# A hybrid decoder step on one Trainium2 core: up-projection of 19 tile pairs by seven products of quarters

## The chip, the core and the metric

The kernel runs on one core of one Trainium2 chip. The engines' names here are those of the profile: PE is the matrix engine (PEld its weight loads), DVE the vector engine, ACT the activation engine, POOL the general engine, SP the engine that issues most of the DMAs. The metric is device time in microseconds (us). The kernel before takes 2202.07 us, the median of three runs (2200.95 to 2202.59).

## The reference

One layer of a decoder trunk is computed for two groups of requests that share weights: a prompt of 1024 tokens and eight samples of one token each. All is float32, the model width is 1024, the feed-forward width FF is 2816. Cut to the part that changes:

```python
def conv_ffn(x, buf, w_up, conv_w, conv_b, w_down):
    L = x.shape[1]
    hup = x @ w_up                                  # 1024 -> 5632
    ext = concatenate([buf, hup], axis=1)
    c = ext[:, 0:L]*conv_w[0] + ext[:, 1:L+1]*conv_w[1] + ext[:, 2:L+2]*conv_w[2] + conv_b
    a, b = split(c, 2, axis=-1)                     # 2816 and 2816
    return (gelu(a) * b) @ w_down, ext[:, -2:]

x = layer_norm(ALPHA*x + mix)                       # mix: mLSTM, pooling and memory attention, gated, @ w_o
f, cbuf_new = conv_ffn(x, cbuf, ...)
x = layer_norm(ALPHA*x + f)
```

Ahead of it stand the memory's keys and values, one input projection with a chunked mLSTM, causal pooling and cross-attention, three gated output projections and the projection `w_o`. The prompt's and the samples' new states are outputs too, among them the last rows of `hup`.

## The kernel before

Activations lie transposed, features on the 128 partitions and TT = 1032 tokens (1024 of the prompt, 8 samples) along a row. Each float32 number is held as a high part that the matrix engine takes in full and a low part with the rest: the normalised stream is `xhi` and `xlo`, eight tiles of 128 features each. A product of two such numbers takes three matmuls (high x high, high x low, low x high).

The main work is a list of `Unit`s. A unit makes 128 output features: for each of three token chunks (`CHUNKS`, 384, 384 and 264 columns) it adds `nk` x 3 matmuls into one PSUM bank at L250 and then calls `evac`, which takes the result out. Weights come as `Split`s of 512 KB: `load` fetches one on SP's queue into a `raw` buffer (L171), `split_part` makes its high part on ACT (L180) and its low part on DVE or POOL (L181), in two halves. `raw` has two buffers, `whi` and `wlo` three each. `run_units` writes the order of all this out by hand: it counts an estimated time per matmul, puts weight halves between matmuls (`tick`), and lets side work (generators in two lanes of `Side`, and `post`, the rest of a unit's evacuation) advance by the same clock. The order in which instructions are written is the order on each engine.

Lines that the texts below touch: L366 is a small step of the layer norms on POOL, L384 to L387 (`to_features`) normalise into `xhi` and `xlo`, L1106 and L1127 store gate and attention chunks to DRAM from POOL's queue, L1375 and L1379 (`wo_unit`) add the stream to the output projection, L1392 transposes that back into rows.

In the feed-forward part an `up_unit` makes one of 44 tiles of 128 columns of `x @ w_up`. ACT writes the rows to `hup` (L1479) and, scaled, to `cv` (L1480). Four steps on DVE add the two other taps of the convolution (L1492, two over the prompt, two over the samples). The first half of the columns then goes through the gelu (L1495), the second half is multiplied with it on POOL (L1498), and the gated row is split into high and low parts (`GH`), which stay in on-chip memory. The up-projection runs by two tiles at a time. The down-projection is cut into groups of four gated rows (`down(j0, 4)`), which are put between the up-units as the rows become ready; each adds into `Z2` (L1533). The last group of four goes by three passes over the tokens (`PASSES`), and the last layer norm (L1597 to L1619) follows each pass.

The tile pool `rows` (`H`, 21 buffers of 1032 columns) holds nearly all larger intermediate tiles. Two kinds of PSUM buffers exist: five of tag `s` (`PS`) and three of tag `d`.

Of the kernel before, what the change touches and what calls it, by code (L numbers as in the profile page):

```python
# [15 lines left out]
T = 1024  # L16
# [13 lines left out]
NEG = -1e30  # L30

# [75 lines left out]
def tile_hybrid_step(ctx: ExitStack, tc: tile.TileContext, x_prompt, mem_prompt, x_sample, cache_mem_k,  # L107
# [9 lines left out]
    wp = ctx.enter_context(tc.tile_pool(name="weights", bufs=2))  # L117
    hp = ctx.enter_context(tc.tile_pool(name="rows", bufs=NH))
# [64 lines left out]
    def run_units(first_loads):  # L183
# [80 lines left out]
        flush()  # L264
# [84 lines left out]
    sp = ctx.enter_context(tc.tile_pool(name="small", bufs=4))  # L349

# [26 lines left out]
    def to_features(rows, c0, n, g0, b0, wait, per=1):  # L377

        for f in range(8):
# [6 lines left out]
            nc.vector.tensor_copy(xhi[:, f, c0:c0 + n], tmp[:, :n])  # L386
# [713 lines left out]
    def gate_unit(b, f, split, col, spill):  # L1100
        def evac(ci, c0, n, p):
            bias = bias_in(GT0 + 8 * b + f)
            if spill:
                t = chunk_tile()
                nc.scalar.activation(t[:, :n], p[:, :n], AF.Identity, bias=bias)  # L1105
                nc.gpsimd.dma_start(GD[b][f][:, c0:c0 + n], t[:, :n])  # L1106
# [16 lines left out]
    def xo1_unit(f, split, col):  # L1123
        def evac(ci, c0, n, p):
            t = chunk_tile()
            nc.scalar.activation(t[:, :n], p[:, :n], AF.Copy)
            nc.gpsimd.dma_start(y1D[f][:, c0:c0 + n], t[:, :n])  # L1127
        return Unit(split, col, 4, mov_o(0), evac)

    def xo2_unit(f, split, col):  # L1130
# [5 lines left out]
        def evac(ci, c0, n, p):  # L1136
# [3 lines left out]
            if ci == 2:  # L1140
                nc.gpsimd.dma_start(mixD[0][f], Y1.pop(f))
# [221 lines left out]
    Z = {}  # L1363
# [4 lines left out]
    def wo_unit(chunk, tiles, f, split, col):  # L1368
        def evac(ci, c0, n, p):
            if tiles[-1] not in Z:  # L1370
                for t in tiles:
                    Z[t] = H(f"z{t}")[:, :1024].rearrange("p (f t) -> p f t", f=8) if t < 8 else \
                        cur[0].tile([128, 8, NS], F32, tag="zs", bufs=1, name="zs")
            tmp = cur[0].tile([128, 392], F32, tag="tmp", bufs=3, name=nm("ztmp"))
            nc.vector.scalar_tensor_tensor(tmp[:, :n], raw_f(xhi[:, f, c0:c0 + n]), ALPHA, p[:, :n], op0=OP.mult,  # L1375
                                           op1=OP.add)
            for t in tiles:
                a, m = t * 128, rows_of(t)
                nc.vector.scalar_tensor_tensor(Z[t][:, f, :], raw_f(xlo[:, f, a:a + m]), ALPHA,  # L1379
                                               tmp[:, a - c0:a - c0 + m], op0=OP.mult, op1=OP.add)  # L1380
        return Unit(split, col, 8, mov_mix, evac, chunks=(chunk,))

    XN = {}

    def g_rows1(tiles):
        st = {}
        for i in range(len(tiles) + 1):
            if i < len(tiles):
                t, m = tiles[i], rows_of(tiles[i])
                p = [PS(), PS()]  # L1390
                for f in range(8):
                    nc.tensor.transpose(p[f // 4][:m, (f % 4) * 128:(f % 4 + 1) * 128], Z[t][:, f, :], ident)  # L1392
                st[t] = p, *ln_stats([q[:m] for q in p], m)
                Z.pop(t)
# [12 lines left out]
    def few_to_features(rows):  # L1407
# [4 lines left out]
        for f in range(8):  # L1412
            nc.scalar.activation(tmp[:, f], p[:, f * NS:(f + 1) * NS], AF.Identity,
                                 bias=colA[:, L1B + f:L1B + f + 1], scale=colA[:, L1G + f:L1G + f + 1])
        nc.vector.tensor_copy(xhi[:, :, T:], tmp)
        nc.vector.tensor_sub(xlo[:, :, T:], tmp, raw_f(xhi[:, :, T:]))

    def g_ln1(tiles):
# [4 lines left out]
        yield from to_features([(XN[t], 128) for t in tiles], tiles[0] * 128, len(tiles) * 128, L1G, L1B, 1.5)  # L1423
# [4 lines left out]
    for i, (chunk, tiles) in enumerate(PASSES):  # L1428
        pairs = list(enumerate(weight_pairs(w_o[0], 0, 1024)))[::-1 if i % 2 else 1]
        for j, (f, sc) in enumerate(pairs):  # L1430
            if i == 0 or j >= NW:
                wo[f] = sc
                sc[0].pool = i+j>1 and (i < 2 or j % 3)
# [3 lines left out]
        on(units[-1], "after", lambda t=tiles, i=i: (side.add(0, f"rows1{i}", g_rows1(t)),  # L1437
# [4 lines left out]
    CA, GH, RW = {}, {}, {}  # L1442
    Z2 = {}
    STT = {}
    TL = {}

    def g_state_conv():

        stT = STT[0] = H("stT")[:, :704].rearrange("p (f j b) -> p f j b", f=44, j=2)
# [8 lines left out]
        for q, (n, t) in enumerate(rows):  # L1458
# [3 lines left out]
            nc.vector.tensor_copy(stT[:, q * 8:q * 8 + n].rearrange("p f j b -> p (f j b)"), p[:, :n * 16])  # L1462
# [219 lines left out]
```

## Time and profile before

| | |
|---|---|
| median of three runs | 2202.07 us |
| the profiled execution, its own time | 2202.02 us |
| its span, first to last instruction | 2200.3 us |
| busy: PE, DVE, ACT, POOL | 2159.7, 1170.9, 797.5, 362.1 us |
| mean granted clock of the matrix engine | 0.995 |
| moved by DMA, mean rate | 229.52 MB, 104 GB/s |

Busy shares are of the whole span. A row of a group of instructions gives the line, engine, operation, what it writes and reads, the shapes, how many there are, their busy time and the mean of one in ns, then the idle time of the engine just ahead of them with what ended it. A row of the timeline gives start and duration in us, and in brackets the idle time ahead and what ended it. Matmuls start before the one ahead of them has drained, so the distance from start to start is what one takes of the engine's time.

### The profile page before, as it was taken

How to read it: one execution, taken by the hardware profiler on the slowest of the kernel's cores; microseconds unless marked ns; L12 is line 12 of the kernel's file. 1: busy time of each engine (PE TensorE's matmuls, PEld its weight loads, DVE VectorE, ACT ScalarE, POOL GpSimd, SP SyncE). 2: the span in 40 equal slices, each digit the busy share in tenths (PEclk: the TensorE clock that was granted, in tenths of full speed). 3: DMA queues.
4: the chain of work that ended last, by engine and by line, in shares of the span. 5: the costliest groups of instructions: out<-in, count | busy, mean ns of one | idle time of the engine just before them, and what ended most of it. 6: DMA issues, size and time to landing. Idle time of an engine off the chain costs nothing.

```text
span 2200.3 us, 35980 instructions
## 1 busy us (share of the span) xinstructions
PE 2159.7 (98%) x14345; PEld 2118.7 (96%) x14345; DVE 1170.9 (53%) x2692; ACT 797.5 (36%) x1583; POOL 362.1 (16%) x523
## 2 busy tenths in 40 slices
PE   8999999999999999999999999999999999999996
PEld 7899999999998999999999999999999999999996
DVE  6844838383856654524335556745544343443457
ACT  5524343434445533332213333544142331423411
POOL 6301010101110000111004633101010110101104
PEclk9999999999999999999999999999999999999998
DMA  8231232323268665659543232311111111111112
GB/s 256 65 107 53 54 69 62 63 53 79 87 175 271 192 207 183 202 184 349 184 140 122 68 88 76 87 49 49 49 39 52 46 49 48 39 58 40 49 49 78
DMA packets 268948, 229.52 MB, mean 104 GB/s; under 512 B 15797, under 2 KB 245991, under 8 KB 268763
## 3 DMA queue, kind: packets, MB, share of 16 engines
q1 hardware_dynamic: 262443, 208.12, 32.0%
q0 software_dynamic: 6336, 19.09, 2.3%
q8 instruction: 113, 1.85, 0.4%
q14 instruction: 56, 0.46, 0.1%
HBM read 177.13 MB, written 50.64 MB: 104 GB/s over the span
## 4 chain that ended last, share of the span: by engine, by line
PE 87%; DVE 4%; issue 4%; POOL 3%; DMA 1%; ACT 1%; SPq 0%; POOLq 0%; ACTq 0%; DVEq 0%
PE pd L250 78%; PE ps L669 2%; PE ps L668 1%; PE ps L670 1%; POOL ps L1276 1%; DVE xlo L387 1%; PE ps L692 1%; DMA Cs<-in_state_C_dram 1%; PE ps L382 0%; DVE xhi L386 0%; PE ps L873 0%; PE ps L1072 0%; DVE st L358 0%; DMA x<-in_x_prompt_dram 0%; POOL mx L1325 0%
## 5 line engine op out<-in xcount | busy, mean ns | idle before, releaser
L250 PE MATMUL pd<-xhi,whi 128*128 128x384 f32 (+1 forms) x2784 | 898.7, 323 | 0.7 <-ACT gf L541 0.7
L250 PE MATMUL pd<-xlo,whi 128*128 128x384 f32 (+1 forms) x2784 | 894.6, 321 | 0.0
L250 PE MATMUL pd<-xhi,wlo 128*128 128x384 f32 (+1 forms) x2784 | 891.1, 320 | 0.0
L250 PEld LDWEIGHTS pd<-xhi,whi 128*128 128x128 f32 x2784 | 523.8, 188 | 10.3 <-issue 8.3
L250 PEld LDWEIGHTS pd<-xlo,whi 128*128 128x128 f32 x2784 | 524.2, 188 | 1.8 <-issue 1.7
L250 PEld LDWEIGHTS pd<-xhi,wlo 128*128 128x128 f32 x2784 | 523.6, 188 | 1.8 <-issue 1.7
L181 DVE TENSOR_TENSOR wlo<-raw,whi 128x512 fp32r<-128x512 f32 (+1 forms) x326 | 227.0, 731 | 440.7 <-ACT whi L180 432.7
L180 ACT ACTIVATE whi<-raw 128x512 fp32r<-128x512 f32 (+1 forms) x382 | 219.3, 619 | 275.8 <-PE pd L250 206.0
L1479 ACT ACTIVATE hup<-pd 128x384 f32<-128x384 f32 (+1 forms) x132 | 60.5, 458 | 276.5 <-PE pd L250 276.4
L1492 DVE SCALAR_TENSOR_TENSOR cv<-hup,colB,cv 128x1023 f32<-128x1023 f32 x88 | 112.7, 1281 | 1.6
L1533 DVE TENSOR_TENSOR z<-pd,z 128x384 f32<-128x384 f32 (+3 forms) x120 | 59.6, 511 | 82.5 <-PE pd L250 82.5
L366 POOL TENSOR_TENSOR rs<-rs,half 128x1 f32<-128x1 f32 (+2 forms) x60 | 38.0, 633 | 340.8 <-DVE rs L365 331.8
L1489 POOL COPY tl<-hup 128x10 f32<-128x10 f32 x44 | 8.4, 192 | 519.2 <-ACT hup L1479 519.2
L1480 ACT ACTIVATE cv<-pd,colB 128x384 f32<-128x384 f32 (+1 forms) x132 | 83.6, 633 | 0.0
L181 POOL TENSOR_TENSOR wlo<-raw,whi 128x512 fp32r<-128x512 f32 x56 | 76.3, 1386 | 41.7 <-ACT whi L180 41.7
L1106 POOL DMA_DIRECT2D gD<-ch x60 | 32.8, 547 | 287.7 <-ACT ch L1105 268.0
L1498 POOL TENSOR_TENSOR cv<-cv,cv 128x1032 f32<-128x1032 f32 x22 | 53.2, 2418 | 112.5 <-DVE cv L1492 96.9
L250 PE MATMUL pd<-mh,whi 128*128 128x392 f32 (+2 forms) x192 | 62.6, 326 | 0.6 <-ACT mh L1327 0.6
L250 PE MATMUL pd<-ml,whi 128*128 128x392 f32 (+2 forms) x192 | 62.0, 323 | 0.1
L1105 ACT ACTIVATE ch<-pd,colA 128x384 f32<-128x384 f32 (+1 forms) x60 | 32.8, 546 | 79.5 <-PE pd L250 59.8
L250 PE MATMUL pd<-mh,wlo 128*128 128x392 f32 (+2 forms) x192 | 61.5, 320 | 0.0
L662 ACT ACTIVATE hh<-ps,colA 128x128 fp32r<-128x128 f32 x64 | 23.1, 361 | 79.7 <-DVE hh L663 75.1
(724 smaller groups left out, 3926.6 us busy)
## 6 DMA issues: line engine op xcount, KB each, us to landing
raw<-in_w_in_dram SPq DMA_DIRECT2D x72, 512.0 KB
raw<-in_w_up_dram SPq DMA_DIRECT2D x44, 512.0 KB
raw<-in_w_down_dram SPq DMA_DIRECT2D x22, 512.0 KB
raw<-in_w_o_dram SPq DMA_DIRECT2D x18, 512.0 KB
mx<-mixD SPq DMA_DIRECT2D x16, 516.0 KB
raw<-in_w_mem_kv_dram SPq DMA_DIRECT2D x16, 512.0 KB
Cs<-in_state_C_dram SPq DMA_DIRECT2D x32, 256.0 KB
out_dram<-Cs SPq DMA_DIRECT2D x32, 256.0 KB
```

The costliest lines, as they stand in the source:

```text
L180: nc.scalar.activation(s.hi[:, ks], s.raw[:, ks], AF.Copy)
L181: (nc.gpsimd if s.pool else nc.vector).tensor_sub(s.lo[:, ks], s.raw[:, ks], raw_f(s.hi[:, ks]))
L250: nc.tensor.matmul(p[:u.m, :n], lhsT=a, rhs=b, start=j == 0, stop=j == len(seq) - 1)
L366: nc.gpsimd.tensor_tensor(out=rs[:n], in0=rs[:n], in1=half[:n], op=OP.pow)
L669: nc.tensor.matmul(out, lhsT=wh, rhs=xl, start=False, stop=False)
L1105: nc.scalar.activation(t[:, :n], p[:, :n], AF.Identity, bias=bias)
L1106: nc.gpsimd.dma_start(GD[b][f][:, c0:c0 + n], t[:, :n])
L1479: nc.scalar.activation(rw[:, c0:c0 + n], p[:, :n], AF.Copy)
L1480: nc.scalar.activation(cc[:, c0:c0 + n], p[:, :n], AF.Identity, bias=colB[:, 132 + ft:133 + ft], scale=colB[:, 88 + ft:89 + ft])
L1492: nc.vector.scalar_tensor_tensor(a, b[0], b[1], a, op0=OP.mult, op1=OP.add)
L1498: nc.gpsimd.tensor_mul(cc, CA.pop(j), cc)
L1533: nc.vector.tensor_add(Z2[f][:, cs], p[:, :n], Z2[f][:, cs])
```

## The change

The up-projection of the first three pairs of column tiles stays as it is. A pair is a tile of the gelu half and the tile of the other half at the same place. For the other 19 pairs the product of a pair is taken as a 2 x 2 block product: the activations in four quarters (512 features x 516 tokens each), the pair's weights in four quarters (512 features x 128 columns). Seven products of sums of quarters take the place of eight products of quarters; the results are put together in PSUM, by adding products onto a bank (`onto`), and on DVE.

- The three sums of activation quarters that the stream itself doesn't hold (products 6, 7, 4) and one that replaces a quarter of it (product 5) are formed once by `g_parts` and `last_part`, from a copy of the normalised stream that `to_features` now also spills to DRAM (`x1D`).
- The sums of weight quarters are formed per pair by DMA: SP loads the first quarter of a sum, and POOL issues accumulating DMAs for the others onto the same tile (`load_weights`): two for product 6, one for 7, one for 5, three for 3. Twelve such tiles exist. `prepare` splits a finished one (256 KB) into high and low parts in one of up to ten buffers.
- `run_pairs` runs the products of half the tokens at a time in the order `ORDER`, with the third and fourth product of a half put among those of the next; `conv_pair` is the convolution of a pair, in seven steps.
- Gated rows go to DRAM (`gD`) and are read back. The down-projection runs as one block after all pairs, in groups of the same sizes as before, with the gated rows of two groups at a time in `xhi` and `xlo`. The residual is read back from `x1D`.
- Ahead of the feed-forward part: weights and raw buffers share one tag of eight buffers; the weights of `w_o` are all split on DVE; the stream's sum in `wo_unit` takes two steps per tile and chunk; the high part in `to_features` moves from DVE to ACT; the stores of gate and attention chunks and the small loads move from POOL's queue to ACT's, one more from POOL's to SP's. The DMA scratch of POOL's queue is 4096 bytes instead of the default.

The core of the diff:

```diff
+NSTD = 3
+SEQ = (1, 2, 6, 7, 5, 3, 4)
+HB, HT = 258, 516
+NWF = 12
...
-    wp = ctx.enter_context(tc.tile_pool(name="weights", bufs=2))
-    hp = ctx.enter_context(tc.tile_pool(name="rows", bufs=NH))
+    wp = ctx.enter_context(tc.tile_pool(name="weights", bufs=8, side="right"))
+    hp = early.enter_context(tc.tile_pool(name="rows", bufs=NH))
...
-            nc.vector.tensor_copy(xhi[:, f, c0:c0 + n], tmp[:, :n])
+            if spill:
+                nc.scalar.dma_start(spill[f][:, c0:c0 + n], tmp[:, :n])
+            nc.scalar.activation(xhi[:, f, c0:c0 + n], tmp[:, :n], AF.Copy)
...
+    def load_weights():
+        for d, chain in list(chains):
+            nc.gpsimd.dma_start(d, chain.pop(0), accum_op=OP.add)
+            if not chain:
+                chains.remove((d, chain))
+        while made["load"] < len(wq) and made["live"] < NWF:
+            o = wq[made["load"]]
+            key = o.steps[made["key"]]
+            first, *chain = o.src[key]
+            o.f[key] = wf_tile(first.shape[1] * 128)
+            d = o.f[key].rearrange("p (k c) -> p k c", c=128)
+            nc.sync.dma_start(d, first)
+            if chain:
+                chains.append((d, chain))
+            made["live"] += 1
...
+    def prepare():
...
+        if key not in o.f or any(d.tensor is o.f[key].tensor for d, _ in chains):
+            return False
+        slot = slots.pop(0)
+        t = (wp if slot == "w" else place["ex"]).tile([128, 1024], F32R, tag="w", name=nm("whl"))
...
+        nc.scalar.activation(hi, src, AF.Copy)
+        nc.vector.tensor_sub(lo, src, raw_f(hi))
...
+        load_weights()
+        return True
...
+            src = {1: (a11,), 2: (a12,), 6: (a21, a22, a11), 7: (a11, a21), 5: (a21, a22),
+                   3: (a12, a21, a22, a11), 4: (a22,)}
...
+        def product(self, m):
+            u = self.u
+            ready_weights(u.w, m)
+            onto = {6: 1, 5: 1, 3: 1, 4: 7}.get(m)
+            if onto is None:
+                self.bank[m] = pp.tile([128, 512], F32, tag="d", bufs=3, name=nm("pd")) if m == 1 else PS("pd")
+            p = self.bank[onto or m][:, :HB]
+            wh, wl = u.w.w[m][:2]
+            for k in range(4):
+                xh, xl = x_part(m, k, self.s)
+                for n, (a, b) in enumerate(((wh, xh), (wh, xl), (wl, xh))):
+                    nc.tensor.matmul(p, lhsT=a[:, k], rhs=b, start=onto is None and k + n == 0,
+                                     stop=k == 3 and n == 2, skip_group_check=onto is not None)
+            if self.s:
+                release(u.w, m)
+            if m in (1, 6, 5):
+                t = small({1: "t1", 6: "u2", 5: "v"}[m])
+                nc.scalar.activation(t, p, AF.Copy)
+                setattr(self, f"s{m}", t)
+            elif m == 2:
+                nc.vector.tensor_add(self.rows(0)[:, self.c1], p, self.s1)
+            elif m == 3:
+                nc.scalar.activation(self.rows(0)[:, self.c2], p, AF.Copy)
+            elif m == 4:
+                nc.vector.scalar_tensor_tensor(self.rows(1)[:, self.c1], p, -1.0, self.s6, op0=OP.mult, op1=OP.subtract)
+        def c22(self):
+            nc.vector.scalar_tensor_tensor(self.rows(1)[:, self.c2], self.bank[7][:, :HB], -1.0, self.s5, op0=OP.mult,
+                                           op1=OP.subtract)
...
+    ORDER = ((1, 0), (2, 0), (3, 1), (6, 0), (4, 1), (7, 0), (5, 0))
+    def run_pairs():
+        before = None
+        halves_ = [Half(u, s) for u in pairs for s in range(2)]
+        for i, h in enumerate(halves_ + [None]):
...
+            for x, (m, old) in enumerate(ORDER):
+                hh = before if old else h
+                if hh is None:
+                    continue
+                hh.product(m)
+                if before and (x == 0 or h is None and m == 3):
+                    before.c22()
+                if m == 4 and hh.s:
+                    post.append(conv_pair(hh.u.j, hh.u.out))
+                if x in (2, 3, 5, 6):
+                    post[:] = [g for g in post if next(g, g) is not g]
+                if x in (0, 1, 4) or x == 3 and h and h.s:
+                    if not prepare():
+                        load_weights()
+                if i == len(halves_) - 1:
+                    early_stage(m)
+                side.advance(12 * HB / 2180.0)
+            before = h
...
+    def stage_split(gi, k, c0, c1):
+        kk = (gi % 2) * 4 + k
+        nc.scalar.activation(xhi[:, kk, c0:c1], stage[gi][:, k, c0:c1], AF.Copy)
+        nc.vector.tensor_sub(xlo[:, kk, c0:c1], stage[gi][:, k, c0:c1], raw_f(xhi[:, kk, c0:c1]))
...
+    pairs = [Pair(j) for j in range(NSTD, NFF)]
...
     run_units(2)
+    made["open"] = True
+    side.finish("parts")
+    slots.extend("www")
+    last_part()
+    load_weights()
+    run_pairs()
+    for u in downs:
+        run_down(u)
+    flush()
...
-    nc = _bacc.Bacc("TRN2", target_bir_lowering=False, num_devices=1)
+    nc = _bacc.Bacc("TRN2", target_bir_lowering=False, num_devices=1, dynamic_dma_scratch_size=4096)
```

Not shown: `early_stage` reads the first four gated rows back during the last half of the last pair, in pieces of 516 columns, and splits them into `xhi` and `xlo`, four while its last products run and four behind the last one that reads those columns; `g_stages` loads and splits the later groups; `run_down` has the same matmuls per group as `down_unit` before.

More of the change, by code (lines that the diff above doesn't have):

```diff
@@ L1414, in few_to_features @@
                                  bias=colA[:, L1B + f:L1B + f + 1], scale=colA[:, L1G + f:L1G + f + 1])
+        for f in range(8):
+            nc.scalar.dma_start(x1D[f][:, T:], tmp[:, f])
         nc.vector.tensor_copy(xhi[:, :, T:], tmp)
@@ L1473, in evac @@
                 box["n"] = 0
[L1474 to L1481 removed]
+                box["r"] = R("hup")
@@ new lines, in last_part, with g_first @@
+    def last_part():
+        for k in range(4):
+            h, l = xhi[:, k, HT:], xlo[:, k, HT:]
+            nc.scalar.activation(h, N1[k], AF.Copy)
+            nc.vector.tensor_sub(l, N1[k], raw_f(h))
+        made["live"] -= 4
+    def g_first():
+        yield 4.0
+        while not made.get("open"):
+            if not prepare():
+                load_weights()
+            yield 3.0
+    on(units[n0 + 4], "before", open_ffn)
+    on(units[-1], "before", lambda: slots.extend("wwwww"))
@@ new lines, in small, with __init__, rows @@
+    def small(s):
+        return place["st"].tile([128, HB], F32, tag=s, bufs=2 if s == "u2" else 1, name=nm(s))
+    class Half:
+        def __init__(self, u, s):
+            self.u, self.s = u, s
+            self.c1, self.c2 = slice(s * HB, (s + 1) * HB), slice(HT + s * HB, HT + (s + 1) * HB)
+            self.bank = {}
+        def rows(self, i):
+            if self.u.out is None:
+                self.u.out = [R("hup"), R("hup")]
+            return self.u.out[i]
+        def product(self, m):
[6 more added lines that the diff above has]
+            wh, wl = u.w.w[m][:2]
+            for k in range(4):
+                xh, xl = x_part(m, k, self.s)
[17 more added lines that the diff above has]
+                                           op1=OP.subtract)
@@ new lines, in conv_pair, with begin, tap @@
+    def conv_pair(j, out):
+        if j % 2 == 0:
+            TL[j // 2] = sp.tile([128, 4, 10], F32, tag="tl", bufs=2, name=nm("tl"))
+        tl = TL[j // 2]
+        c = {}
+        def begin(i):
+            ft = j + NFF * i
+            c[i] = R("cv")
+            nc.scalar.activation(c[i], out[i], AF.Identity, bias=colB[:, 132 + ft:133 + ft],
+                                 scale=colB[:, 88 + ft:89 + ft])
+            nc.scalar.activation(tl[:, 2 * i + j % 2, :], out[i][:, T - 2:], AF.Copy)
+        def tap(i, far):
+            ft = j + NFF * i
+            w = colB[:, 44 * (1 - far) + ft:44 * (1 - far) + ft + 1]
+            n = 1 + far
+            for a, b in ((c[i][:, n:T], out[i][:, :T - n]), (c[i][:, T:], stT[:, ft, 1 - far, :])):
+                nc.vector.scalar_tensor_tensor(a, b, w, a, op0=OP.mult, op1=OP.add)
+        begin(0)
+        yield
+        tap(0, 0)
+        yield
+        tap(0, 1)
+        begin(1)
+        yield
+        tap(1, 0)
+        nc.scalar.activation(c[0], c[0], AF.Gelu_apprx_tanh)
+        yield
+        tap(1, 1)
+        yield
+        nc.vector.tensor_mul(c[1], c[0], c[1])
+        yield
+        if j % 2:
+            kept_rows(j)
+        nc.sync.dma_start(gD[j], c[1])
@@ L1580, in tile_hybrid_step @@
+    pairs = [Pair(j) for j in range(NSTD, NFF)]
+    downs = []
+    for gi in range(5):
+        downs += [Down(gi, f, down_weights(gi, f)) for f in range(8)]
+    downs[0].before = lambda: side.add(0, "stages", g_stages())
     gb = {}
```

426 lines of the change are left out of this document (291 added, 135 removed).

## The prediction

> **What bounds the kernel now.** I read the page first, then the chain of work that ended last, then the windows and rows of the stage that changes.
>
> ```profile
> span 2200.3 us, 35980 instructions
> ...
> PE 2159.7 (98%) x14345; PEld 2118.7 (96%) x14345; DVE 1170.9 (53%) x2692; ACT 797.5 (36%) x1583; POOL 362.1 (16%) x523
> ...
> PE pd L250 78%; PE ps L669 2%; PE ps L668 1%; PE ps L670 1%; POOL ps L1276 1%; DVE xlo L387 1%; PE ps L692 1%; DMA Cs<-in_state_C_dram 1%; PE ps L382 0%; DVE xhi L386 0%; PE ps L873 0%; PE ps L1072 0%; DVE st L358 0%; DMA x<-in_x_prompt_dram 0%; POOL mx L1325 0%
> ```
>
> The matmul line L250 holds 78% of the chain. A busy PE alone proves little, since matmuls overlap in the records; so I look at the chain and the window of the feed-forward part.
>
> ```profile
> 1516.54 90.62 PE pd L250 x576
> ...
> 1881.29 45.28 PE pd L250 x288
> ```
> ```profile
> 1429.90:2140.00 710.10, 708.68 (x4493) 706.38 (x4493) 318.75 (x489) 240.37 (x428) 61.26 (x64) 1.00 0.16 48
> ```
>
> In that window (columns: PE, weight loads, DVE, ACT, POOL, then clock, DMA share, GB/s) PE runs without a gap at clock 1.00, DVE is busy 45% (318.75 of 710.10), ACT 34%, POOL 9%, DMA 16%. Chain pieces are unbroken PE: 576 matmuls in 90.62 us, in triples of 384, 384 and 264 columns, so 0.472 us a triple. Only fewer or shorter matmuls make this stretch shorter, and there is room beside them. What counts is the spacing of starts:
>
> ```profile
> 1389.76 0.28 PE L250 MATMUL pd<-mh,wlo 128*128 128x256 f32 x1
> ...
> 1390.83 0.28 PE L250 MATMUL pd<-mh,wlo 128*128 128x256 f32 x1
> ...
> 2097.60 0.28 PE L250 MATMUL pd<-xhi,whi 128*128 128x264 f32 x1
> ...
> 2098.94 0.28 PE L250 MATMUL pd<-xhi,wlo 128*128 128x264 f32 x1
> ```
>
> The first two are 9 steps apart: 118.9 ns for 256 columns. The others are 11 steps apart: 121.8 ns for 264.
>
> **Matmuls of the 19 pairs (the gain).** A pair is two column tiles of up-projection: 2 x 24 triples x 0.472 = 22.65 us. Changed: seven products x 4 k x 3 x 2 halves = 168 matmuls of 258 columns, which is 43,344 streamed columns against 49,536. Between the two spacings 258 columns take 119.6 ns, so 20.09 us a pair. Saved: 2.56 x 19 = **48.6 us**. With 121.8 ns for all it is 41.6, with 118.9 ns 50.8. The three unsplit pairs and the down-projection have the same matmuls as before, in another order: 0.
>
> **DVE and ACT in a pair.** These must stay under 20.09 us to be hidden.
>
> ```profile
> L181 DVE TENSOR_TENSOR wlo<-raw,whi 128x512 fp32r<-128x512 f32 x318 | 219.9, 726 | 434.8 <-ACT whi L180 426.8 <-PE pd L250 5.2 <-DMA ck<-in_cache_mem_k_dram 0.7
> L180 ACT ACTIVATE whi<-raw 128x512 fp32r<-128x512 f32 x374 | 216.4, 624 | 275.8 <-PE pd L250 206.0 <-issue 41.0 <-DMA raw<-in_w_o_dram 14.0
> L1492 DVE SCALAR_TENSOR_TENSOR cv<-hup,colB,cv 128x1022 f32<-128x1022 f32 x44 | 56.5, 1283 | 1.6
> L1495 ACT ACTIVATE cv<-cv 128x1032 f32<-128x1032 f32 x22 | 23.5, 1068 | 22.7 <-DVE cv L1492 22.7
> L1533 DVE TENSOR_TENSOR z<-pd,z 128x264 f32<-128x264 f32 x32 | 13.7, 429 | 19.6 <-PE pd L250 19.6
> L733 DVE SCALAR_TENSOR_TENSOR C<-C,dec,ps 128x258 f32<-128x258 f32 x56 | 24.4, 478 | 5.8 <-PE ps L670 5.5
> L1492 DVE SCALAR_TENSOR_TENSOR cv<-stT,colB,cv 128x8 f32<-128x8 f32 x88 | 19.7, 224 | 1.5
> L1479 ACT ACTIVATE hup<-pd 128x264 f32<-128x264 f32 x44 | 17.2, 391 | 64.6 <-PE pd L250 64.6
> ```
>
> DVE: seven splits 7 x 0.726 = 5.08; the tap steps 4 x 1.283 + 4 x 0.224 = 6.03; two adds from PSUM 0.86 and four subtractions 1.91; the gating product, which leaves POOL, costed like a tap, 1.28. Sum 15.2 us, 75% of 20.09. ACT: splits 4.37, eight evacuations 3.13, two scalings and a gelu at 1.068 are 3.20, and kept rows, at most two copies of 0.391 and a little, 0.9: 11.6 us, 58%. PE has no work by itself there, so they stay hidden if no wait is too late. The tightest are on the banks of products 1 and 7: a later product adds onto a bank only after ACT has copied it, and two other products (2.9 us) lie in between, against 0.391 us for the copy and at most 1.07 ahead of it. In the second half of each pair nearly all tap steps fall, some 10 us of DVE in 10 us; the first half has about 5, and weights are prepared about three products ahead, so it recovers. Cost 0; bound +1 us a pair.
>
> **The accumulating DMAs (the unknown).** Each pair issues seven plain loads of 256 KB on SP and seven accumulating ones from POOL, two for product 6, one each for 7 and 5, three for 3. An accumulation must wait for the one before it on the same tile, and that wait stands in POOL's in-order queue, with all later accumulations behind it. The trace has none; nearest are POOL's stores.
>
> ```profile
> L1106 POOL DMA_DIRECT2D gD<-ch x60: 539/539/620, 570.6 to 1049.0; - x60
> ```
> ```profile
> gD<-ch POOLq DMA_DIRECT2D x40, 192.0 KB, 4.1
> ...
> mixD<-y1r POOLq DMA_DIRECT2D x8, 516.0 KB, 6.1
> ...
> y1D<-ch POOLq DMA_DIRECT2D x16, 192.0 KB, 2.9
> ```
>
> Issuing takes g = 0.54 us for 128 rows; landing L is 2.9 to 6.1 us. Three accumulations a pair wait for a landing, four follow without: a period of 3L + 4g. Low end, 3 x 2.9 + 4 x 0.54 = 10.9 us. High end, 6.1 and four times the issue time for four times the rows: 3 x 6.1 + 4 x 2.2 = 26.9. By size, 256 KB lies between 4.1 and 6.1 at 4.5, and I take twice the issue time: 3 x 4.5 + 4 x 1.08 = 17.8 us, under 20.09. It is the nearest row that I go by (192 KB). Twelve buffers are 12/7 pairs of lead, 34 us, which also absorb the first lateness. Cost 0.
>
> The Trainium skill, "DMA: Bandwidth & Descriptors", section "Anatomy of one DMA — SWDGE (gpsimd) path", fits one such DMA as 2.0 us plus bytes over 436e3, 2.6 us for 256 KB; the sum by it would be 10.0 us a pair, and the rows of 192 KB at 2.9 and 4.1 are longer, so the rows decide.
>
> The 16 DMA engines are the second bound.
>
> ```profile
> 15.00:20.00 5.00, 5.00 (x42) 5.00 (x43) 4.02 (x10) 3.21 (x7) 4.15 (x4) 1.00 1.09 353
> ```
>
> 353 GB/s at full share, and 48 at 0.16 above (300 at full), put 256 KB at 0.74 to 0.87 us; seven loads are 6.1 at most, and a gated row's store of 516 KB 1.8. Accumulations at the price of a load make 14.0 us, at twice (they read both terms) 20.1, at three times 26.2. I take something under twice.
>
> **Into the pairs.** During four unsplit units (4 x 24 x 0.472 = 45 us) the sums of the activation quarters are formed.
>
> ```profile
> L660 DVE TENSOR_TENSOR CH<-C,CH 128x516 fp32r<-128x516 f32 x28 | 19.5, 697 | 5.8 <-ACT CH L659 5.8
> ```
>
> Sixteen sums and twelve splits (4 k) at 0.697 are 19.5 us of DVE; the four units themselves cost 8 half-splits, taps and products: 8 x 0.726 + 8 x 1.283 + 8 x 0.224 + 2 x 1.28 = 20.4. Together 39.9 of 45 us, just hidden, apart from the four last splits (2.8 us), needed four products in. The reload of x waits for ACT's spills and for the row buffers to be closed. I take +3 us, bounds 0 and +12.
>
> **Into the down-projection.** Eight pieces of gated rows come back from DRAM during the last half, 8 x 0.697 = 5.6 us on a DVE that has 10 to do in 10 there; PE has two products (2.9 us) and one chunk (2.1) before it needs the late four. +2 us, bounds 0 and +8. Later groups have 45 us (the 288 matmuls above) for their load and split: 0.
>
> **The small moves, together.**
>
> ```profile
> L181 POOL TENSOR_TENSOR wlo<-raw,whi 128x512 fp32r<-128x512 f32 x56 | 76.3, 1386 | 41.7 <-ACT whi L180 41.7
> L1379 DVE SCALAR_TENSOR_TENSOR z<-xlo,ztmp 128x128 f32<-128x128 f32 x64 | 25.1, 443 | 0.6
> L386 DVE CAST xhi<-tmp 128x384 fp32r<-128x384 f32 x32 | 18.0, 563 | 4.9 <-ACT tmp L384 4.9
> ```
> ```profile
> 1408.89 0.33 PE L1392 MATMUL ps<-ident,z 128*128 128x128 f32 x1 [2.40 <-DVE z L1379]
> ```
>
> Around the output projection DVE takes over some 28 half-splits from POOL (28 x 0.726 = 20 us), and loses 64 short z steps (28 us) for 24 longer ones of about a cast's 0.563 (14) and the casts (18, now on ACT): 12 us less in all. The spills and small loads go from POOL's queue to ACT's, behind its in-order work; SP's queue now waits for one shared pool of eight weight buffers, freed by PE, but three units (34 us) ahead. All that lies under PE; the one gap to win is the 2.40 us. 0, bounds -3 and +6.
>
> **Sum** against the profiled execution: 2200.3 - 48.6 + 3 + 2 = 2156.7 us of span; outside its span that execution had 2202.02 - 2200.3 = 1.7, so 2158.4. It stands with the median of the runs, 2202.07. Own range of this case: 2149 (best spacing, no hand-over costs, the gap won) to 2170.
>
> **Rivals.**
> 1. *Slower: POOL's waits or accumulating packets set the pace.* At L = 6.1 and g = 1.5 the period is 24.3 us; 19 x (24.3 - 20.09) = 80, less some 20 of lead, on 2158: 2218 us. At 26.9 it would be near 2267. It decides from about 23.4 us a pair, (48.6 - 5 + 20) / 19 over 20.09. For it: nothing here shows an accumulation, and twice a load's price already fills the DMA engines. Against it: the nearest landing. Chance 0.22.
> 2. *The same in a mild form, or DVE late in each second half*: a period of 21 to 23 us, 19 x 1.5 = 28 less a part of the lead: about 2178. Chance 0.21. POOL's own work can stretch beside DVE:
>
> ```profile
> 216.91 0.19 POOL L647 COPY smpT<-k 128x8 f32<-128x8 f32 x1 [4.30 <-ACT k L640]
> ...
> 234.50 0.58 POOL L647 COPY smpT<-v 128x8 f32<-128x8 f32 x1 [0.90 <-DVE v L643]
> ```
>
>    The same copy takes 0.19 or 0.58 us. If each issue waited out a tap of 1.28, 4 x (0.54 + 1.28) + 13.5 = 20.8 us a pair, 13 us in all. The Trainium skill, "SBUF — State Buffer", section "Who interferes with whom", says that copies, casts and tensor-scalar operations of DVE can lock GpSimd out of a shared port; the pair's DVE list above has none of these, and POOL's store issues at 539 to 620 ns agree.
> 3. *The change doesn't do what it says:* short matmuls fall to the pace of weight loads.
>
> ```profile
> L250 PEld LDWEIGHTS pd<-xhi,whi 128*128 128x128 f32 x2784 | 523.8, 188 | 10.3 <-issue 8.3
> ```
>
>    168 x 0.188 would be 31.6 us a pair, near 2377. That 256 columns follow each other at 118.9 ns, with a load each, speaks against it: 0.01.
> 4. *No measurable change*, between 1 and 2: 0.03.
>
> **How the numbers follow.** The forecast has 0.53, and the predicted time is its 2158 us. A measurement of this kernel tells about 0.2% (4.4 us) from no change. Faster by more: 0.53 + 0.21 = 0.74; within: 0.03; slower: 0.22 + 0.01 = 0.23. The range 2149 to 2225 leaves out about 0.05 below and 0.13 above, the worse part of rival 1.
>
> **What would show it.** Right: unbroken chains of 168 matmuls at 20.1 us a pair, spacing near 119.6 ns, DVE near 75% and DMA share at 0.7 to 0.9 there, and POOL idle part of each pair. Wrong: PE waiting for a weight split whose ACT copy waits for an accumulating DMA, POOL's queue waiting without a break, a landing over 6 us; or gaps of over 10 us where the pairs begin and end; or a DVE without idle time in the pairs.

## The result: 4.4% slower, and the profile after

The changed kernel takes 2298.5 us (median; 2294.3 to 2300.7) where the kernel before, on the same chip, takes 2201.8: a ratio of 1.0437 [1.0424, 1.0449]. The forecast was 2158 with a range up to 2225, so it failed on the wrong side, in the way of rival 1. The profiled execution took 2299.1 us, its span 2297.0.

The page after, the lines that answer to those shown of before:

```profile
span 2297.0 us, 37937 instructions
...
PE 2162.7 (94%) x14801; PEld 2117.2 (92%) x14801; DVE 1245.2 (54%) x2822; ACT 854.5 (37%) x1717; POOL 381.2 (17%) x462
...
q0 software_dynamic: 70224, 34.87, 12.4%
...
PE pd L258 46%; PE pd L1926 10%; DMA wf<-in_w_up_dram 9%; POOL wf L1567 3%; PE pd L1743 2%; PE ps L675 1%; PE ps L676 1%; PE ps L677 1%; PE ps L699 1%; DMA ck<-in_cache_mem_k_dram 1%; DMA Cs<-in_state_C_dram 1%; DVE wlo L189 1%; POOL ps L1283 1%; ACT whl L1598 1%; PE ps L387 1%
...
wf<-in_w_up_dram POOLq DMA_DIRECT2D x133, 256.0 KB, 6.2
```

L1743 are the matmuls of the seven products, and they hold 2% of the chain in a stage that lasts 502.5 us. In their place stand the transfers of `wf` (9%), for the most part the accumulating DMAs, and the POOL line that issues them; an accumulation lands 6.2 us after its issue (the last row, a median). The window of the pairs, from the first seven-product matmul to the first of the down-projection (columns as before: PE, weight loads, DVE, ACT, POOL, clock, DMA share, GB/s):

```profile
1505.50:2008.00 502.50, 425.81 (x3230) 421.07 (x3229) 260.93 (x430) 202.94 (x406) 163.97 (x126) 0.90 0.87 166
```

That is 502.5 / 19 = 26.45 us a pair, where 20.09 were forecast and 22.65 were taken before. No engine is full: PE 85%, DVE 52%, ACT 40%, POOL 33%. Such a stage is paced by waits, and the list of waits names their links (us in total, times, longest):

```profile
POOL wf L1567 <- DMA wf<-in_w_up_dram: 269.3, 57, 8.9
...
ACT whl L1598 <- DMA wf<-in_w_up_dram: 196.0, 33, 13.0
...
PE pd L1743 <- ACT u L1749: 71.4, 17, 7.4
...
POOL wf L1567 <- issue: 37.1, 13, 5.1
```

57 waits are three a pair: the second accumulation of product 6, the second and third of product 3. In the window of the pairs alone, 55 of them last 257.7 us, and POOL's waits for DVE, which frees the buffers, 14.2 us in 4, so the twelve buffers hold it little. POOL's timeline over two pairs shows how they set the period:

```profile
1711.39 1.28 POOL L1567 DMA_DIRECT2D wf<-in_w_up_dram  x1 [5.03 <-DMA wf<-in_w_up_dram]
1716.42 2.60 POOL L1567 DMA_DIRECT2D wf<-in_w_up_dram  x2 [3.75 <-DMA wf<-in_w_up_dram]
1723.41 3.93 POOL L1567 DMA_DIRECT2D wf<-in_w_up_dram  x3 [4.39 <-DMA wf<-in_w_up_dram]
1729.24 1.29 POOL L1567 DMA_DIRECT2D wf<-in_w_up_dram  x1 [1.90 <-issue]
1736.92 1.28 POOL L1567 DMA_DIRECT2D wf<-in_w_up_dram  x1 [6.39 <-DMA wf<-in_w_up_dram]
1743.04 2.62 POOL L1567 DMA_DIRECT2D wf<-in_w_up_dram  x2 [4.83 <-DMA wf<-in_w_up_dram]
1750.26 3.91 POOL L1567 DMA_DIRECT2D wf<-in_w_up_dram  x3 [4.61 <-DMA wf<-in_w_up_dram]
1757.95 1.31 POOL L1567 DMA_DIRECT2D wf<-in_w_up_dram  x1 [3.78 <-issue]
```

```profile
L1567 POOL DMA_DIRECT2D wf<-in_w_up_dram x133: 1273/1301/2439, 1474.2 to 1979.8; - x133
```

(the last row, from the view of the tile: shortest, median and longest issue in ns, and when the first and last started). The pattern of 1, 2, 3, 1 issues repeats after 25.5 us (1711.39 to 1736.92). Of these, 9.1 are issues, the rest waits: POOL is idle 64% of the time and yet never free, since a wait at the head of its in-order queue holds all later accumulations back. What ends such a wait is the landing of POOL's own transfer: in the chain of work that ended last, the piece `DMA wf` of 7.29 us begins with the issue at 1729.24 and ends ahead of the one at 1736.92.

The way from there to PE goes through ACT's in-order queue, not through the weights directly:

```profile
1721.08 1.15 ACT L1598 ACTIVATE whl<-wf 128x512 fp32r<-128x512 f32 x2 [8.54 <-DMA wf<-in_w_up_dram]
1722.14 0.36 ACT L1754 ACTIVATE hup<-pd 128x258 f32<-128x258 f32 x1
...
1722.88 0.36 ACT L1749 ACTIVATE u<-pd 128x258 f32<-128x258 f32 x1
```
```profile
1723.29 0.58 PE L1743 MATMUL pd<-xhi,whl 128*128 128x258 f32 x1 [3.63 <-ACT u L1749]
```

The split of a weight sum stands 8.5 us at the head of ACT's queue; the copy `u`, which PE needs before it may add onto that bank, stands behind it. So PE is reported as waiting for ACT, though ACT itself was waiting for the accumulations.

Where the 140.3 us between the span summed (2156.7) and the span seen (2297.0) lie: 120.8 in the pairs (502.5 against 19 x 20.09); 12.2 ahead of the feed-forward part, whose first matmul starts late:

```profile
1404.83 0.28 PE L250 MATMUL pd<-xhi,whi 128*128 128x264 f32 x1
```
```profile
1417.05 0.28 PE L258 MATMUL pd<-xhi,whi 128*128 128x264 f32 x1
```

(before, then after); and 7.3 in the rest, beyond the 5 that the sum had for the two hand-overs. Of the hand-over into the down-projection, the wait at the end of the last pair (4.7 us) is counted with the pairs.

### The profile page after: what moved, and what is told of

Same layout as the page of the kernel before. It is cut to its first block, busy times and chain, and to the rows that moved or that the text cites. A ratio compares the mean times of both kernels' runs of the same rounds, so it can differ in the third digit from the quotient of the medians.

```text
span 2297.0 us, 37937 instructions
## 1 busy us (share of the span) xinstructions
PE 2162.7 (94%) x14801; PEld 2117.2 (92%) x14801; DVE 1245.2 (54%) x2822; ACT 854.5 (37%) x1717; POOL 381.2 (17%) x462
## 3 DMA queue, kind: packets, MB, share of 16 engines
q0 software_dynamic: 70224, 34.87, 12.4%
## 4 chain that ended last, share of the span: by engine, by line
PE 67%; DMA 11%; issue 7%; DVE 5%; POOL 4%; ACT 3%; SPq 0%; ACTq 0%; POOLq 0%; DVEq 0%
PE pd L258 46%; PE pd L1926 10%; DMA wf<-in_w_up_dram 9%; POOL wf L1567 3%; PE pd L1743 2%; PE ps L675 1%; PE ps L676 1%; PE ps L677 1%; PE ps L699 1%; DMA ck<-in_cache_mem_k_dram 1%; DMA Cs<-in_state_C_dram 1%; DVE wlo L189 1%; POOL ps L1283 1%; ACT whl L1598 1%; PE ps L387 1%
## 5 line engine op out<-in xcount | busy, mean ns | idle before, releaser
L258 PE MATMUL pd<-xhi,whi 128*128 128x384 f32 (+1 forms) x1872 | 607.0, 324 | 6.3 <-ACT hup L1524 6.3
L258 PE MATMUL pd<-xlo,whi 128*128 128x384 f32 (+1 forms) x1872 | 604.1, 323 | 0.0
L258 PE MATMUL pd<-xhi,wlo 128*128 128x384 f32 (+1 forms) x1872 | 601.1, 321 | 0.0
L258 PEld LDWEIGHTS pd<-xhi,whi 128*128 128x128 f32 x1872 | 353.4, 189 | 15.8 <-issue 8.3
L258 PEld LDWEIGHTS pd<-xlo,whi 128*128 128x128 f32 x1872 | 353.3, 189 | 1.8 <-issue 1.7
L258 PEld LDWEIGHTS pd<-xhi,wlo 128*128 128x128 f32 x1872 | 353.2, 189 | 1.8 <-issue 1.7
L1743 PE MATMUL pd<-xhi,whl 128*128 128x258 f32 x1216 | 258.4, 309 | 71.9 <-ACT u L1749 71.4
L1743 PEld LDWEIGHTS pd<-xhi,whl 128*128 128x128 f32 x1216 | 217.5, 215 | 75.6 <-ACT u L1749 74.9
L1926 PE MATMUL pd<-xhi,whl 128*128 128x384 f32 (+3 forms) x1056 | 252.0, 325 | 9.4 <-DVE z L1936 5.1
L1567 POOL DMA_DIRECT2D wf<-in_w_up_dram x133 | 173.3, 1603 | 381.8 <-DMA wf<-in_w_up_dram 269.3
L1926 PEld LDWEIGHTS pd<-xhi,whl 128*128 128x128 f32 x1056 | 186.4, 191 | 10.9 <-DVE z L1936 6.2
L1743 PE MATMUL pd<-xlo,whl 128*128 128x258 f32 x608 | 186.7, 307 | 0.0
L1743 PE MATMUL pd<-tx,whl 128*128 128x258 f32 x1368 | 172.6, 284 | 4.7 <-DVE hup L1759 4.7
L1743 PEld LDWEIGHTS pd<-tx,whl 128*128 128x128 f32 x1368 | 167.8, 190 | 5.3 <-DVE hup L1759 5.0
L1743 PEld LDWEIGHTS pd<-xlo,whl 128*128 128x128 f32 x608 | 131.2, 216 | 0.0
```

Of the source, the lines that this page charges most:

```text
L258: nc.tensor.matmul(p[:u.m, :n], lhsT=a, rhs=b, start=j == 0, stop=j == len(seq) - 1)
L1567: nc.gpsimd.dma_start(d, chain.pop(0), accum_op=OP.add)
L1743: nc.tensor.matmul(p, lhsT=a[:, k], rhs=b, start=onto is None and k + n == 0, stop=k == 3 and n == 2, skip_group_check=onto is not None)
L1926: nc.tensor.matmul(p[:, :n], lhsT=a[:, k], rhs=b, start=k + i == 0, stop=k == nk - 1 and i == 2)
```

## The experiments

Times without an interval are of a single execution, on a chip where the kernel before took 2203.2 us (the first four kernels below) or 2202.3 us (the others). The theories that the expectations speak of: W1, the chained waits in POOL's queue set the pace; W2, the work of the accumulations on the 16 DMA engines sets it; beside them stands the pause named "issue" in POOL's queue, laid to a descriptor scratch of 4096 bytes.

### No accumulations

```diff
-            src = {1: (a11,), 2: (a12,), 6: (a21, a22, a11), 7: (a11, a21), 5: (a21, a22),
-                   3: (a12, a21, a22, a11), 4: (a22,)}
+            src = {1: (a11,), 2: (a12,), 6: (a21,), 7: (a11,), 5: (a21,), 3: (a12,), 4: (a22,)}
```

> Leaves all accumulating DMAs out: each of the seven weight tiles of a pair holds one quarter, not its sum, so the products 6, 7, 5 and 3 are of other numbers. Theory W (accumulating DMAs set the pace of the pairs): the pair falls from 26.4 to 20.1 us, PE without gaps at clock 1.00 there, time near 2299 - 19 x 6.3 = 2179 us. Rival D (DVE is late or the hand-over waits dominate): the pair stays above 22.6 us and the time above 2225.

2184.9 us, span 2183.0. The window of the pairs, and the chain within it:

```profile
1502.90:1897.30 394.40, 389.11 (x3231) 387.83 (x3230) 258.91 (x429) 204.29 (x405) 0.00 (x0) 0.99 0.42 129
```
```profile
1545.06 0.44 PE ps L1509 x4
1545.49 40.32 PE pd L1742 x336
1585.82 0.44 PE ps L1509 x4
```

108.1 us of the pairs go with the accumulations alone, and the period is 20.76 us, a little over the 20.1 expected. In the chain, 336 matmuls of two pairs follow each other unbroken at 120.0 ns, 20.16 us a pair. The window also says how the 108.1 were lost: PE is idle 5.3 us here and 76.7 in the changed kernel (71.4 more, the sum of its waits for `u`), and the same matmuls are 36.7 us longer there (425.81 against 389.11), at a clock of 0.90 against 0.99. The clock follows PE's stops: in the changed kernel it is 0.50 in 17 stretches of the pairs, 101 us in all, and each begins during one of PE's waits (2.7 to 7.4 us) or less than 1 us behind it. Two windows of the changed kernel, behind the wait of 3.63 us shown above:

```profile
1723.30:1729.50 6.20, 6.20 (x29) 6.20 (x30) 2.95 (x6) 2.73 (x6) 4.19 (x4) 0.50 0.98 227
1729.50:1746.40 16.90, 16.90 (x141) 16.75 (x140) 9.00 (x14) 5.45 (x11) 4.93 (x4) 1.00 0.85 146
```

Without accumulations PE is busy for all of the 370 us from 1510 to 1880, at clock 1.00. No run changes the stops alone, so that they lower the clock is read from this order in time.

With the sums left out, the changed kernel is 18 us under the kernel before, not 44.

### Seven accumulations a pair, none chained

One addition onto each of the seven tiles, so as many accumulations as in the change, with no wait for another one:

```diff
+            src = {1: (a11, a12), 2: (a12, a11), 6: (a21, a22), 7: (a11, a21), 5: (a21, a22),
+                   3: (a12, a21), 4: (a22, a21)}
```

> The same seven plain loads and seven accumulating DMAs a pair, but one accumulation on each of the seven tiles, so none waits for another one on its own tile (sums of other quarters than the reference's). Theory W1 (the three chained waits in POOL's in-order queue set the pace): 7 x 1.3 to 1.6 us of issue fit in 20.1, time near 2180 to 2200. Rival W2 (the DMA engines, share 0.89, are full): share x period = 23.5 us of engine time a pair stays, so the period stays at 23 to 26 us and the time at 2235 to 2300.

2200.9 us. The window of its pairs, and its page:

```profile
1513.50:1909.50 396.00, 389.93 (x3231) 388.08 (x3230) 260.35 (x429) 205.16 (x405) 161.54 (x125) 0.99 1.11 212
```
```profile
q0 software_dynamic: 70224, 34.87, 12.8%
...
wf<-in_w_up_dram POOLq DMA_DIRECT2D x133, 256.0 KB, 6.8
```

20.84 us a pair, the same as without any. POOL issues 125 of the 133 accumulations in these 396 us, the share of the DMA engines is 1.11, and they land even later than in the change (6.8 against 6.2 us). So neither the amount nor a landing by itself sets the pace: it takes accumulations that wait for each other. W2 falls. Of the 16.0 us more than without accumulations, 1.6 lie in the pairs, 10.6 ahead of them (PE's one wait there for ACT's `hup` is 12.9 us instead of 6.2) and 3.8 behind them.

### A larger descriptor scratch

```diff
-    nc = _bacc.Bacc("TRN2", target_bir_lowering=False, num_devices=1, dynamic_dma_scratch_size=4096)
+    nc = _bacc.Bacc("TRN2", target_bir_lowering=False, num_devices=1, dynamic_dma_scratch_size=5888)
```

> The accumulating DMAs as in the changed kernel, the DMA scratch of POOL's queue 5888 bytes instead of 4096. Theory R (the 1.9 to 4.5 us pauses ahead of one issue in each pair, and its 2.4 instead of 1.3 us, are a full descriptor ring): one pause a pair goes or shrinks, up to 19 x 3 = 57 us less, time 2240 to 2280. Rival (the pause is a wait for a load or the landing): no change, 2290 to 2305.

2293.7 us, 26.32 us a pair. The pause "issue" (37.1 us in 13 times) is gone from POOL's waits, and the others have grown by 49.0:

```profile
POOL wf L1567 <- DMA wf<-in_w_up_dram: 318.3, 56, 10.1
```

The scratch was a real cause of a real pause, and worth little or nothing here (2293.7 against 2294.3 to 2300.7, where 2240 to 2280 was expected): landing rose from 6.2 to 7.0 us, and the time only changed its name. 3 x 7.0 + 4 x 1.30 is 26.2 us without a pause, against the 26.32 measured.

### The same sums with four accumulations

Products 5 and 6 hold sums that 6 and 3 need: tile 5 is a21 + a22, tile 6 is a11 more. So one accumulation each, two of them from a tile that already lies on chip (the kernel also keeps 11 tiles in use instead of 12):

```diff
-            src = {1: (a11,), 2: (a12,), 6: (a21, a22, a11), 7: (a11, a21), 5: (a21, a22),
-                   3: (a12, a21, a22, a11), 4: (a22,)}
+            src = {1: (a11,), 2: (a12,), 5: (a21, a22), 6: (a11, 5), 7: (a11, a21), 3: (a12, 6), 4: (a22,)}
...
-            nc.gpsimd.dma_start(d, chain.pop(0), accum_op=OP.add)
+            s = chain.pop(0)
+            nc.gpsimd.dma_start(d if len(s.shape) == 3 else d.rearrange("p k c -> p (k c)"), s, accum_op=OP.add)
```

> All sums as in the changed kernel, with four accumulating DMAs a pair instead of seven: the sum for product 5 is added onto product 6's tile from on-chip memory, and that onto product 3's. Two chained waits are left. Theory W1: 2 x 6.2 + 2 x 1.3 = 15 us a pair, under PE's 20.1, time near 2180. Theory W2: four accumulations of 2.1 us and 7.9 us of loads and stores are 16.3 us, also under 20.1. If a chained wait with an on-chip source is much longer than 6.2 us (10 or more), the pair stays at 23 us and above: 2235 or more.

2186.1 us: within 1.2 us of the kernel with no accumulation at all, each a single execution. Its window, the groups on POOL, and its DMA list:

```profile
1503.60:1899.80 396.20, 389.40 (x3231) 387.90 (x3230) 259.01 (x429) 203.76 (x404) 79.31 (x72) 1.00 0.77 179
```
```profile
L1570 POOL DMA_DIRECT2D wf<-in_w_up_dram x38 | 53.7, 1412 | 180.0 <-DMA wf<-in_w_up_dram 71.5 <-ACT hup L1524 47.1 <-DVE whl L1605 39.2
...
L1570 POOL DMA_DIRECT2D wf<-wf x38 | 33.6, 885 | 155.5 <-DMA wf<-in_w_up_dram 64.1 <-DVE whl L1605 25.4 <-DVE cv L1786 18.7
```
```profile
wf<-in_w_up_dram POOLq DMA_DIRECT2D x38, 256.0 KB, 5.8
wf<-wf POOLq DMA_DIRECT2D x38, 256.0 KB, 4.6
```

20.85 us a pair. Two accumulations a pair still wait for another one, so chaining as such does no harm: it does when the chain's waits and issues add up to more than PE's period. Here POOL waits also for DVE to free a buffer (`whl`), which is the sign of a queue that is ahead.

### Plain loads in the same chains

The 133 transfers on POOL's queue stay with all their waits, but overwrite instead of adding.

```diff
-            nc.gpsimd.dma_start(d, chain.pop(0), accum_op=OP.add)
+            nc.gpsimd.dma_start(d, chain.pop(0))
```

> The changed kernel with its 133 POOL transfers as plain loads: each overwrites the tile with the next quarter, in the same chains and with the same waits, so the weight sums are left out. It measures the accumulation by itself. If the landing of any POOL load and POOL's queue make the 26.4 us a pair, landing stays near 6 us and the time within 2270 to 2300. If the accumulation does (packets that read both terms), landing falls to 4 us or less, the period 3L + 4g to 3 x 4 + 4 x 1.3 = 17.2 us, and the time to about 2185.

2194.6 us. Its window, its group on POOL, and its page:

```profile
1505.90:1901.60 395.70, 389.39 (x3231) 387.88 (x3230) 258.56 (x428) 204.33 (x405) 93.69 (x126) 1.00 0.71 211
```
```profile
L1567 POOL DMA_DIRECT2D wf<-in_w_up_dram x133 | 99.1, 750 | 344.7 <-DMA wf<-in_w_up_dram 278.9 <-ACT hup L1524 48.8 <-ACT xhi L1689 15.7
```
```profile
q0 software_dynamic: 10640, 34.87, 5.4%
...
wf<-in_w_up_dram POOLq DMA_DIRECT2D x133, 256.0 KB, 5.1
```

20.83 us a pair. The landing of a plain load, expected at 4 us or less, was 5.1: even that guess was low. With 0.75 us an issue, 3 x 5.1 + 4 x 0.75 = 18.3 us by the medians, under PE's period. But POOL's queue is not far ahead, as its waits in the pairs and ACT's show:

```profile
POOL wf L1567 <- DMA wf<-in_w_up_dram: 266.4, 54, 9.3
...
ACT whl L1598 <- DMA wf<-in_w_up_dram: 37.7, 18, 6.0
```

POOL waits nearly three times a pair for a landing, as in the change, and ACT in nearly every pair; PE is idle only 6.3 us of the stage, against 5.3 without the transfers. So the sum by the medians is too low here: the plain chain just keeps pace, and the accumulating one, at 26.45 us a pair, does not. What an addition has over a load: 528 packets a transfer against 80 (70224 and 10640 over 133); 2.1 us of all 16 DMA engines against 0.9 (12.4% of 2297.0 and 5.4% of 2192.6, over 133); a median of 1.30 us an issue against 0.75; and 6.2 us to landing against 5.1.

### The sums on DVE, and on POOL

Four quarter loads a pair and four additions by an engine, ahead of the splits; the second kernel has `nc.gpsimd` instead, and makes the fourth sum one product earlier.

```diff
+            src = {"A": a11, "B": a12, "C": a21, "E": a22}
...
+        nc.vector.tensor_add(f["S"], f["C"], f["E"])
+        nc.vector.tensor_add(f["C"], f["A"], f["C"])
+        nc.vector.tensor_add(f["A"], f["S"], f["A"])
...
+                add(f["B"], f["A"], f["B"])
```

> No accumulating DMAs: the four quarters of a pair's weights are loaded once each by SP, and the four sums are formed by four adds on DVE (128x512, some 0.7 us each), reusing one another. DVE would be busy 15.2 + 2.8 = 18.0 of 20.1 us a pair. Theory W1 (only the chained waits were too slow): PE-bound, the pair at 20.8 us as without accumulations, time near 2185. Rival (DVE is the next bound, its second half of each pair being full already): 21.5 us or more a pair, time 2200 or more.

> As the kernel before in this list, with the four adds on POOL (1.386 us each beside DVE in the trace of before), one split earlier. 4 x 1.39 = 5.5 us of POOL a pair, none of DVE. Theory W1: the pair at 20.8 us, time near 2185. Rival (DVE and POOL, both with two inputs from on-chip memory, hold each other up: 15.2 + 5.5 = 20.7 us one after the other): 21 to 22.5 us a pair, time 2190 to 2215.

2198.5 us with DVE, 2213.4 with POOL; 21.51 and 22.28 us a pair. The rivals had it, not W1, though the first time stays just under the rival's 2200. The windows:

```profile
1503.10:1911.80 408.70, 397.10 (x3230) 389.44 (x3229) 304.28 (x504) 204.48 (x405) 0.00 (x0) 1.00 0.29 91
```
```profile
1503.70:1927.00 423.30, 399.91 (x3230) 390.80 (x3230) 326.59 (x428) 205.36 (x405) 145.78 (x76) 0.99 0.28 87
```

The second one looks odd: DVE has lost its additions, 428 instructions to 504, and is busier, 326.6 us to 304.3. The groups say why. First a small step on DVE in the kernel with no accumulations, then the same step with the sums on POOL, then two of POOL's own additions there:

```profile
L1780 DVE SCALAR_TENSOR_TENSOR cv<-stT,colB,cv 128x8 f32<-128x8 f32 x76 | 16.9, 222 | 0.0
```
```profile
L1818 DVE SCALAR_TENSOR_TENSOR cv<-stT,colB,cv 128x8 f32<-128x8 f32 x76 | 67.8, 892 | 0.0
```
```profile
L1640 POOL TENSOR_TENSOR wf<-wf,wf 128x512 f32<-128x512 f32 x19 | 41.1, 2163 | 288.8 <-DVE whl L1619 210.7 <-DMA wf<-in_w_up_dram 78.1
...
L1644 POOL TENSOR_TENSOR wf<-wf,wf 128x512 f32<-128x512 f32 x19 | 24.5, 1292 | 24.7 <-DVE whl L1619 24.6
```

A DVE step of 222 ns takes 892 on the mean, and an addition on POOL takes 1.29 or 2.16 us by its place: the two engines stretch each other. The timeline shows both ways. Beside an addition of 2.28 us (from 1715.47) DVE's 8-column steps take 1.27 and 1.25 us; beside one of 1.29 us (from 1720.89) it is DVE's split that takes 1.73 us instead of 0.68. The Trainium skill, "SBUF — State Buffer", section "Who interferes with whom", says that a DVE operation of two tensors that both lie in on-chip memory contends with GpSimd's reads there; these rows agree. With accumulating DMAs nothing of the kind showed: their issues have a median of 1.301 us and a least of 1.273, and DVE is busy 260.9 us with them and 258.9 without.

What follows, from single executions: the sums cost about nothing as four accumulating DMAs (1 us), 14 us on DVE (2198.5 against 2184.9) and 29 on POOL, all far below the 114 of the change's seven.

### A version that mends the other losses

To the kernel with four accumulations: the eight small loads at the start go back from ACT's queue to POOL's, the samples' spill goes to SP's queue, and the first weights of the pairs are split 10 us later.

```diff
-            nc.scalar.dma_start(rowsA[dst:dst + n], as_rows(src))
+            nc.gpsimd.dma_start(rowsA[dst:dst + n], as_rows(src))
...
-            nc.scalar.dma_start(x1D[f][:, T:], tmp[:, f])
+            nc.sync.dma_start(x1D[f][:, T:], tmp[:, f])
...
-        yield 4.0
+        yield 14.0
         while not made.get("open"):
```

> The kernel with four accumulations a pair (2186 us), with three hand-overs mended: the eight small loads at the start back on POOL's queue (PE idle 8.2 us there), the first weight split of the pairs asked for 10 us later, when its weights have landed (PE idle 6.6 us behind ACT's evacuation), and the samples' spill issued by SP instead of ACT (PE idle 3.2 us behind ACT). If these waits are what they seem, 8 + 6.6 + 3 and some clock go: 2165 to 2170. If others take their place: 2175 or more.

2177.6 us, so other waits took their place. The loss ahead of the feed-forward part is gone: its first matmul starts at 1404.87. The loads were its main part: behind the first 24 matmuls of L258, the next starts at 24.45 in the changed kernel and at 15.33 here. In the changed kernel's ACT timeline (ACTq is the queue's own issue; two of the eight shown):

```profile
12.99 0.28 ACTq L319 DMA_DIRECT2D rowsA<-in_ln_g_dram  x1
14.31 0.28 ACTq L319 DMA_DIRECT2D rowsA<-in_ln_b_dram  x1
14.64 1.21 ACT L453 ACTIVATE memT0h<-ps 128x256 fp32r<-128x256 f32 x4 [12.33 <-DMA rowsA<-in_ln_in_g_dram]
```

Each takes 0.28 us to issue, but they leave ACT's queue 1.3 to 1.9 us apart, and the first evacuation of the program stands behind them for 12.3 us (PE loses 8.0 of them). PE's wait for ACT's `hup` at the last unsplit tile, 6.6 us in the kernel with four accumulations, was to go with the later split; it remained at 5.7.

The last version has these edits too: the first sum of the activations 8 us later, the last four pieces of the first gated rows split when the last pair's results are out, and later groups' splits 8 us later.

```diff
         load(0)
-        yield 4.0
+        yield 12.0
         load_weights()
...
             place_piece(3, 0)
+        elif m == 0:
             for k in range(4):
                 place_piece(k, 1)
...
             stage_load(gi, ((0, TT),))
-            yield 8.0
+            yield 16.0
```

> The mended kernel (2178 us) with three more waits moved: the activation quarters are asked for 8 us before the first of them is split (PE idle 5.7 us behind ACT), the four late pieces of gated rows are split behind the last pair's results (PE idle 4.8 us behind DVE), and the second group's gated rows 8 us later (PE idle some 5 us behind DVE, which waits for that load). If each wait is what it seems: 15 us less and some clock, 2160 to 2165. If the loads themselves are late and new waits take their place: 2170 or more.

2175.1 us (2173.5 to 2177.1) against 2201.7 for the kernel before: 0.9882 [0.9866, 0.9899]. It beats the kernel before, but misses the 2160 to 2165 expected, and is hardly under the 2177.6 of the version ahead of it (one execution). Its waits of PE:

```profile
PE pd L1748 <- ACT t L1754: 11.7, 1, 11.7
...
PE pd L1748 <- DVE hup L1764: 2.3, 1, 2.3
```

The wait at the end of the pairs fell from 4.8 to 2.3 us, and the one for `hup` at their beginning vanished, with a longer one in its place: the sums that start later end later, ACT's queue stands 5.7 and 2.8 us for them, and behind them stands the copy `t` of the first product. Moving one piece moved the wait; what bounds this hand-over as a whole stays open.

## Why the prediction was wrong, step by step

- **The step that failed: "The accumulating DMAs (the unknown)".** It put the right mechanism and formula, 3L + 4g, and wrote Cost 0 beside it. L was taken as 4.5 us and is 6.2; g as 1.08 and is 1.30; and a pause of 2.0 us a pair (37.1 / 19) was not in it. With these, 3 x 6.2 + 4 x 1.30 + 2.0 = 25.8 us, against 25.5 in the timeline and 26.45 over the stage. The choice of L went by size from stores of 192 KB. Plain loads of 256 KB in the same chains took 5.1 us, so 0.6 of the missing 1.7 us lie in the transfer without the addition and 1.1 come with the addition; what in it makes them isn't shown. The estimate of 2.6 us by the Trainium skill ("DMA: Bandwidth & Descriptors", section "Anatomy of one DMA — SWDGE (gpsimd) path") lies further off; the prediction had put the rows ahead of it.
- **Rival 1 happened**, named with its place and its point of decision (about 23.4 us a pair). It put 2267 at a period of 26.9. Its 20 us off for the lead did not come: the pairs, which begin at 1505.50, waited almost from there, as the chain of the changed kernel shows:

```profile
1510.16 5.54 DMA wf<-in_w_up_dram
...
1516.45 8.35 DMA wf<-in_w_up_dram
```

  A buffer of lead pays once, and a producer that is slower than its consumer costs in every pair.
- **The second half of rival 1, the DMA engines, was not the cause**, though its price came out: an addition costs 2.4 times a load (2.1 against 0.9 us), above the "something under twice". The rate at which the trace gives a share of 1.0 was taken for the capacity (353 GB/s "at full share" is a row at 1.09), and the unchained kernel ran at 1.11 with PE at full pace: 1.11 x 20.84 is 23.1 us of engine time in a pair of 20.84.
- **Matmuls of the 19 pairs: right.** 120.0 ns against 119.6. To 20.16 us a pair come 0.22 of transposes for the kept rows (0.44 in two pairs), which the sum left out, and 0.25 for the wait of 4.8 at the end: 20.63. The last 0.13 of the 20.76 (2.4 us in all) lie mostly at that end too, where the last 12 matmuls take 2.95 us instead of 1.44.
- **DVE and ACT in a pair: right.** 258.9 of 394.4 us is 66%, ACT 52%, where 75 and 58 were forecast, and no wait of PE on them without accumulations but at the ends.
- **The small moves: wrong by more than their bounds**, 10.6 to 12.2 us against -3 to +6. "Behind its in-order work" had named the queue, but only for what the loads would wait for; who would wait for the loads on ACT's queue was not asked.
- **The hand-overs:** 12.3 us (7.3 and 5) outside the pairs and the start, and 4.7 for the wait at the end of the pairs, where 5 were summed: within the bounds given (0 to +20).
- **What would show it wrong** listed the sight that came: ACT's copy waiting for an accumulating DMA, POOL's queue waiting without a break, a landing over 6 us.

So, had the accumulations cost nothing, as forecast, the time would still have been 2185 (the kernel without them), 27 us over the forecast. In span 26.3: 10.6 for the start (first up-projection matmul at 1415.46), 12.7 for the pairs (20.76 against 20.09), 3.0 for the rest.

## What to carry to other kernels

A chain of transfers that wait for each other on an in-order queue is a recurrence: sum its landings and issues per period, with a landing taken among as many transfers as will be in flight, and compare with the period of the bound engine; if the estimate is near, look first for a version with fewer links (here seven additions became four, by reusing sums, and 112 us came back). When an engine's copy is blamed for a wait, read what stood ahead of it on its queue. Before a DMA is moved to a queue that also computes, ask what it will hold up there.

## What was not expected of the hardware

- An accumulating DMA of 256 KB from DRAM takes 528 packets, a plain one with the same tile and source 80; from an on-chip source 144 (25536 packets for 76 transfers with the four accumulations, less 38 x 528). The on-chip source was also cheaper to issue (0.89 against 1.41 us in that kernel) and earlier to land (4.6 against 5.8).
- The landing of an accumulation from DRAM had medians of 6.2 us in the changed kernel and 6.8 in the unchained one, and PE ran at full pace in the latter alone: by itself it says nothing of the period.
- The share of the DMA engines went to 1.11 over 396 us.
- Eight small loads left ACT's queue 1.3 to 1.9 us apart and blocked its first computation for 12.3 us.
